# Four small edits in an fp32 decoder-layer kernel: v's sums in a paired PSUM buffer, a ninth matmul on ones, the third and fourth input blocks as DMAs of their own, and one weight piece split beside the second norm

## The chip, the core and the metric

The kernel runs on one core of a Trainium2 chip. The metric is the device time of one execution in microseconds (us); the median of several runs counts. The engines are PE (matmul; PEld is its weight load), DVE (VectorE), ACT (ScalarE), POOL (GpSimd) and SP (SyncE), which here issues all the DMAs.

## The reference, cut to what matters

```python
def hybrid_layer(x, ...):                       # x: (1, 256, 1024) float32
    h = rmsnorm(x, norm_mix_g)
    proj = h @ w_in                              # 1024 x (3*512 + 512 + 2*1024)
    q, k, v, u_pool, gate_logits = split(proj)
    q = rotary(rmsnorm(heads(q), q_norm_g)); k = rotary(rmsnorm(heads(k), k_norm_g))
    attn = causal_attention(q, k, heads(v))      # 8 heads of 64; one block of 256
    pooled = multiscale_pool_mixer(u_pool, w_pool, pool_scale)
    gates = sigmoid(gate_logits + b_gate)
    x = x + (gates[0] * (attn @ w_branch_attn) + gates[1] * (pooled @ w_branch_pool)) @ w_out
    h2 = rmsnorm(x, norm_ffn_g)
    gate, val = split(causal_conv3(h2 @ w_up))   # 1024 x 5632
    return x + (silu(gate) * val) @ w_down       # 2816 x 1024
```

All of it is float32. The kernel gets float32 precision by splitting every operand of a large product into a high and a low part and adding three products: high by high, high by low, low by high.

## The kernel before, in words

x is held transposed, 8 blocks k of 128 features by 256 tokens. The host packs block k of x and block k of q's weights side by side (256 + 512 columns a block, tile `xq`), with 8 columns of norm weights in front. A list of DMAs over `XCUTS` (L58, L191 to L196) loads them on SP's queue: blocks 0, 1, then 2-3, 4-5, 6-7. Behind them come k's first weights in two halves, a table `par`, and then whole chunks of 128 x 2048 (1 MB) in the fixed order of `order` (L107 on): k, v, p, g, ..., up, dn. A ring of four raw buffers holds the chunks; the DMA of the next chunk is issued when the last piece of the one in its buffer is split.

**Splitting.** A chunk is split in two pieces of 1024 columns: ACT rounds it (`high`, tile `hi_...`), DVE subtracts (`low`, tile `lo_...`). `ahead()` (L163) issues the next `high` and the next due `low` in the order of the chunks, wherever the program calls it. So the calls of `ahead()` are the plan: one more call moves every later piece one call forward, until the ring of four split buffers stops it (L145).

**Order.** At its end the program adds a dependency between neighbours on each engine, so every engine runs in written order.

**Warm-up.** Before the first data are there, `WARM` float32 matmuls of `ones` by `ones` run (L205). In the profile one of them is two MATMUL rows.

**Projections.** `project` (L274) makes q, k and v token-major: two PSUM banks (two tiles of 128 tokens by 512 columns), 8 blocks, 6 matmuls of 512 columns a block. The banks come from the pool `mm` of four in turn: warm-up, q0, q1, k0, k1, v0, v1, then u and the transposes. A bank is written again only when its readers are done. q0 and q1 are read by `norm_evacuate` (L287): ACT squares `q_q` and the DVE product `qg_q` (L295), which need the token norm `rtok` first. A second pool, `ps2`, has two buffers of two banks each; its first tile `ps_n1` holds the sums of the first norm and their spread (L242, L253), then attention's scores `ps_s` and probabilities `ps_p` use it, and at the end `ps_n2`, the second norm.

**FFN.** For each of 22 feature tiles i: two `ps_up` products (gate, value; 24 matmuls of 256 columns each), `normed`, `taps` and silu on DVE, ACT and POOL, and 24 matmuls of the down product of tile i - 3. Tiles 0 and 1 stand apart because the second norm is not there yet: tile 0 and half of tile 1 run first, `token_rms` (L242), `diagonal` (L249) and `spread_rms` (L253, L254) make `R2`, and only then can DVE empty the banks.

Of the kernel before, what the change touches and what calls it, by code (L numbers as in the profile page):

```python
# [8 lines left out]
F32 = mybir.dt.float32  # L9
# [5 lines left out]
P = 128  # L15
S = 256
NT = S // P
# [27 lines left out]
C_END = C_SIN + NT * ROPE  # L45

LAG = 3
WARM = 8
RAWBUFS = 4
WBUFS = 4  # L50
STAGGER = 1
# [3 lines left out]
FIRST = 2  # L55
HOME = 24
LEAD = 104
XCUTS = (1, 2, 4, 6, 8)  # L58


@with_exitstack
def hybrid_layer_kernel(ctx: ExitStack, tc: tile.TileContext, xq_d, par_d, wkv_d, wpg_d,
# [11 lines left out]
    ps2 = pairs.enter_context(tc.tile_pool(name="ps2", bufs=2, space=bass.MemoryType.PSUM))  # L74
    tmp = mixer.enter_context(tc.tile_pool(name="tmp", bufs=2))

    def bank(name):
        return mm.tile([P, 512], F32, tag="mm", name=name)
# [63 lines left out]
    def next_high():  # L142
        if at[0] < len(pieces):
            c, sl, first, _ = pieces[at[0]]
            if c - oldest() >= WBUFS:  # L145
                return
            at[0] += 1
            if first:
                his[c] = whi_p.tile([P, CH], F32R, tag="whi", name=f"hi_{order[c][0]}{c}")
                los[c] = wlo_p.tile([P, CH], F32R, tag="wlo", name=f"lo_{order[c][0]}{c}")  # L150
            high(his[c][:, sl], raw(c, sl))

    def next_low(eager=False):
        if at[1] < at[0] - STAGGER or at[0] == len(pieces) > at[1] or (at[1] < at[0] and eager):
            c, sl, _, last = pieces[at[1]]
            at[1] += 1
            low(los[c][:, sl], his[c][:, sl], raw(c, sl))
            if last and order[c][0] != "q":
                load()
# [3 lines left out]
    def ahead(upto=0):  # L163

        next_high()
        next_low()
        if at[1] - sum(p[0] < used[0] for p in pieces) < upto:
            next_high()
            next_low()

    def chunk(name):
        c = used[0]
        used[0] += 1
        spent.update(i for i in range(c) if order[i][0] != "dn")
        assert order[c][0] == name and all(p[0] > c for p in pieces[at[1]:]), (name, order[c][0])
        return his[c], los[c]
# [15 lines left out]
    cut = 0  # L192
    for k in XCUTS:
        end = KD + k * (S + AW)
# [9 lines left out]
    warm = bank("ps_warm")  # L204
    for i in range(WARM):  # L205
        nc.tensor.matmul(warm[:, 0:P], ones, ones, start=True, stop=True)
# [40 lines left out]
    def diagonal(rtok):  # L247
        for t in range(NT):
            nc.vector.tensor_scalar(diag[:, t, :], ident, rtok[:, t:t + 1], None, op0=ALU.mult)  # L249

    def spread_rms(pb, R):

        nc.tensor.matmul(pb, ones, diag.rearrange("p t c -> p (t c)"), start=True, stop=True)  # L253
        nc.vector.tensor_copy(R, pb)  # L254
# [16 lines left out]
            nc.vector.tensor_tensor(x2[:, 0:n * S], x2[:, 0:n * S], x2[:, n * S:2 * n * S], ALU.add)  # L271
            n //= 2

    def project(name, hook):  # L274
        pt = [bank(f"ps_{name}{t}") for t in range(NT)]
        for k in range(KD):
            if k % 4 == 0:
                hi, lo = chunk(name)
            sl = slice((k % 4) * 512, (k % 4 + 1) * 512)
            for sx, wx in ((xhi, hi), (xlo, hi), (xhi, lo)):  # L280
                for t in range(NT):
                    nc.tensor.matmul(pt[t], sx[:, k, t * P:(t + 1) * P], wx[:, sl], start=k == 0 and sx is xhi and wx is hi,  # L282
                                     stop=k == KD - 1 and wx is lo)
            hook(k)
        return pt
# [65 lines left out]

    qg, kg, stat = [], [], []
    ptq = project("q", on_q)
    ptk = project("k", on_k)
    ptv = project("v", on_v)
    for t in range(NT):
        nc.scalar.activation(vn[:, t, :], ptv[t], AF.Copy, scale=rtok1[:, t:t + 1])

# [204 lines left out]
    def tile_part(w, opers, c, ps, ks):  # L563
        hi, lo = w
        oph, opl = opers
        for k in ks:
            sl = slice(k * 256 + c * P, k * 256 + (c + 1) * P)
            mm3(ps[:, 0:S], (hi[:, sl], lo[:, sl]), (oph[:, k, :], opl[:, k, :]), k == 0, k == KD - 1)
# [38 lines left out]
    def normed(ps, f, name):  # L607

        u = tmp.tile([P, S], F32, tag="u", bufs=4, name=f"u_{name}")
        nc.vector.tensor_tensor(u, ps[:, 0:S], R2, ALU.mult)  # L610
        c = tmp.tile([P, S], F32, tag="cv", bufs=5, name=f"c_{name}")
        cw = par[:, C_CW + 2 * 2 * KF + f:C_CW + 2 * 2 * KF + f + 1]
        nc.scalar.activation(c, u, AF.Identity, scale=cw, bias=par[:, C_CB + f:C_CB + f + 1])
        return u, c
# [49 lines left out]
    ps = [bank("ps_up1_0")]  # L664
    tile_part(w, (hhi, hlo), 0, ps[0], range(KD))
    diagonal(rtok2)
    spread_rms(stat[:, 1, 0:S], R2)
    ug = normed(ps0[0], 0, "g0")
    uv = normed(ps0[1], KF, "v0")
# [107 lines left out]
```

## Time and profile before

| what | value |
|---|---|
| median of 3 runs | 342.76 us (342.73 to 342.76) |
| the profiled execution | 342.95 us; its span 341.1 us |
| around the span | 1.85 us |
| PE busy | 335.4 us, 98% of the span |
| DVE, ACT, POOL busy | 259.9, 198.1, 87.9 us |
| DMA | 62.76 MB, 184 GB/s mean |
| granted TensorE clock | 1.00 in every slice |

A row of a timeline gives the start from the start of the span, the duration, engine, line, operation, output<-input, shapes and count; in square brackets stands how long the engine was idle before and what ended that. The end of a matmul is modelled, and two matmuls overlap, so for PE the starts are what to compare: the start of the next row minus the start of this one is the time that its matmuls took.

### The profile page before, as it was taken

How to read it: one execution, taken by the hardware profiler on the slowest of the kernel's cores; microseconds unless marked ns; L12 is line 12 of the kernel's file. 1: busy time of each engine (PE TensorE's matmuls, PEld its weight loads, DVE VectorE, ACT ScalarE, POOL GpSimd, SP SyncE). 2: the span in 40 equal slices, each digit the busy share in tenths (PEclk: the TensorE clock that was granted, in tenths of full speed). 3: DMA queues.
4: the chain of work that ended last, by engine and by line, in shares of the span. 5: the costliest groups of instructions: out<-in, count | busy, mean ns of one | idle time of the engine just before them, and what ended most of it. 6: DMA issues, size and time to landing. Idle time of an engine off the chain costs nothing.

```text
span 341.1 us, 6723 instructions
## 1 busy us (share of the span) xinstructions
PE 335.4 (98%) x2736; PEld 324.6 (95%) x2736; DVE 259.9 (76%) x411; ACT 198.1 (58%) x319; POOL 87.9 (26%) x104
## 2 busy tenths in 40 slices
PE   8999999999999999999999999999999999999996
PEld 7887899999899999999999999999999999999995
DVE  4969989797587676698799977777777777777743
ACT  4956544635748954678276675655666666656420
POOL 1007992022203025022232322121212121212130
PEclk9999999999999999999999999999999999999999
DMA  7985543455372652376336674655556464642003
GB/s 266 422 343 225 195 179 121 157 171 219 113 254 110 221 175 102 123 249 246 125 123 218 265 246 142 243 159 213 190 181 223 149 246 133 240 142 107 0 2 123
DMA packets 10254, 62.76 MB, mean 184 GB/s; under 512 B 1136, under 2 KB 2288, under 8 KB 3312
## 3 DMA queue, kind: packets, MB, share of 16 engines
q1 hardware_dynamic: 10224, 62.34, 50.3%
q8 instruction: 21, 0.34, 0.4%
q14 instruction: 9, 0.07, 0.1%
HBM read 61.29 MB, written 1.05 MB: 183 GB/s over the span
## 4 chain that ended last, share of the span: by engine, by line
PE 85%; DVE 6%; DMA 4%; ACT 2%; SPq 1%; issue 1%; POOL 1%; POOLq 0%; ACTq 0%
PE ps_up L95 10%; PE ps_up L96 10%; PE ps_up L94 10%; PE ps_d L640 6%; PE ps_d L639 6%; PE ps_d L641 6%; PE ps_g L94 5%; PE ps_g L95 4%; PE ps_g L96 4%; DMA raw_k<-in_wkv 4%; PE ps_v L282 3%; PE ps_out L95 2%; PE ps_out L94 2%; PE ps_out L96 2%; PE ps_bp L94 1%; PE ps_ba L95 1%
## 5 line engine op out<-in xcount | busy, mean ns | idle before, releaser
L96 PE MATMUL ps_up<-hhi,lo_up 128*128 128x256 f32 x352 | 97.4, 277 | 0.6 <-DVE lo_up L86 0.6
L94 PE MATMUL ps_up<-hhi,hi_up 128*128 128x256 f32 x352 | 97.6, 277 | 0.0
L95 PE MATMUL ps_up<-hlo,hi_up 128*128 128x256 f32 x352 | 97.4, 277 | 0.0
L96 PEld LDWEIGHTS ps_up<-hhi,lo_up 128*128 128x128 f32 x352 | 66.1, 188 | 0.7 <-DVE lo_up L86 0.7
L95 PEld LDWEIGHTS ps_up<-hlo,hi_up 128*128 128x128 f32 x352 | 66.1, 188 | 0.2 <-DVE hlo L88 0.2
L94 PEld LDWEIGHTS ps_up<-hhi,hi_up 128*128 128x128 f32 x352 | 66.1, 188 | 0.0
L86 DVE TENSOR_TENSOR lo_up<-raw_up,hi_up 128x1024 fp32r<-128x1024 f32 x44 | 54.5, 1242 | 6.2 <-ACT hi_up L82 6.2
L639 PE MATMUL ps_d<-ah,hi_dn 128*128 128x256 f32 x176 | 48.6, 276 | 0.0
L640 PE MATMUL ps_d<-al,hi_dn 128*128 128x256 f32 x176 | 48.6, 276 | 0.0
L641 PE MATMUL ps_d<-ah,lo_dn 128*128 128x256 f32 x176 | 48.6, 276 | 0.0
L622 POOL TENSOR_TENSOR c_v<-c_g,c_v 128x256 f32<-128x256 f32 x22 | 16.2, 738 | 118.5 <-DVE c_v L605 118.5
L82 ACT ACTIVATE hi_up<-raw_up 128x1024 fp32r<-128x1024 f32 x44 | 45.0, 1046 | 0.0
L94 PE MATMUL ps_g<-xhi,hi_g 128*128 128x256 f32 x128 | 36.4, 285 | 0.0
L82 ACT ACTIVATE ah<-c_v 128x256 fp32r<-128x256 f32 x22 | 9.2, 418 | 45.8 <-POOL c_v L622 45.8
L96 PE MATMUL ps_g<-xhi,lo_g 128*128 128x256 f32 x128 | 35.7, 279 | 0.0
L95 PE MATMUL ps_g<-xlo,hi_g 128*128 128x256 f32 x128 | 35.7, 279 | 0.0
L641 PEld LDWEIGHTS ps_d<-ah,lo_dn 128*128 128x128 f32 x176 | 33.0, 188 | 0.0
L640 PEld LDWEIGHTS ps_d<-al,hi_dn 128*128 128x128 f32 x176 | 33.0, 188 | 0.0
L639 PEld LDWEIGHTS ps_d<-ah,hi_dn 128*128 128x128 f32 x176 | 33.0, 188 | 0.0
L86 DVE TENSOR_TENSOR lo_dn<-raw_dn,hi_dn 128x1024 fp32r<-128x1024 f32 x22 | 27.8, 1263 | 0.4 <-ACT hi_dn L82 0.4
L610 DVE TENSOR_TENSOR u_v<-ps_up,R 128x256 f32<-128x256 f32 x22 | 9.3, 421 | 22.7 <-PE ps_up L96 22.7
L94 PEld LDWEIGHTS ps_g<-xhi,hi_g 128*128 128x128 f32 x128 | 24.3, 190 | 0.9 <-issue 0.3
(183 smaller groups left out, 805.5 us busy)
## 6 DMA issues: line engine op xcount, KB each, us to landing
raw_up<-in_wup SPq DMA_DIRECT2D x22, 1024.0 KB, 4.8
raw_dn<-in_wdn SPq DMA_DIRECT2D x11, 1024.0 KB, 4.8
raw_g<-in_wpg SPq DMA_DIRECT2D x8, 1024.0 KB, 4.9
raw_o<-in_wout SPq DMA_DIRECT2D x4, 1024.0 KB, 4.8
xq<-in_xq SPq DMA_DIRECT2D x3, 768.0 KB, 7.4
raw_v<-in_wkv SPq DMA_DIRECT2D x2, 1024.0 KB, 14.0
raw_p<-in_wpg SPq DMA_DIRECT2D x2, 1024.0 KB, 6.3
raw_bp<-in_wbp SPq DMA_DIRECT2D x2, 1024.0 KB, 4.8
```

Of the source, the lines that this page charges most:

```text
L82: nc.scalar.activation(hi, src, AF.Copy, scale=scale)
L86: nc.vector.tensor_tensor(lo, src, hi.bitcast(F32), ALU.subtract)
L94: nc.tensor.matmul(out, sh, mh, start=start, stop=False, **kw)
L95: nc.tensor.matmul(out, sh, ml, start=False, stop=False, **kw)
L96: nc.tensor.matmul(out, sl, mh, start=False, stop=stop, **kw)
L282: nc.tensor.matmul(pt[t], sx[:, k, t * P:(t + 1) * P], wx[:, sl], start=k == 0 and sx is xhi and wx is hi, stop=k == KD - 1 and wx is lo)
L610: nc.vector.tensor_tensor(u, ps[:, 0:S], R2, ALU.mult)
L622: nc.gpsimd.tensor_tensor(uc[1], g[1], uc[1], ALU.mult)
L639: nc.tensor.matmul(o, hi[:, sl], acch[i], start=first, stop=False, skip_group_check=True)
L640: nc.tensor.matmul(o, hi[:, sl], accl[i], start=False, stop=False, skip_group_check=True)
L641: nc.tensor.matmul(o, lo[:, sl], acch[i], start=False, stop=i == KF - 1, skip_group_check=True)
```

## The change

Four edits. (1) `WARM` is 9 instead of 8. (2) `XCUTS` loads blocks 2 and 3 each with a DMA of its own. (3) v's two sums lie in one tile `ps_v` of the pool `ps2`, not in two banks of `mm`. (4) One more `ahead()` is called between `diagonal(rtok2)` and `spread_rms` of the second norm. Lines after L355 move by 2, after L666 by 3.

```diff
-WARM = 8
+WARM = 9
...
-XCUTS = (1, 2, 4, 6, 8)
+XCUTS = (1, 2, 3, 4, 6, 8)
...
-    def project(name, hook):
-        pt = [bank(f"ps_{name}{t}") for t in range(NT)]
+    def project(name, hook, pt=None):
+        pt = pt or [bank(f"ps_{name}{t}") for t in range(NT)]
...
-    ptv = project("v", on_v)
+
+    psv = ps2.tile([P, 2, 512], F32, tag="ps2", name="ps_v")
+    ptv = project("v", on_v, [psv[:, t, :] for t in range(NT)])
...
     tile_part(w, (hhi, hlo), 0, ps[0], range(KD))
     diagonal(rtok2)
+    ahead()
     spread_rms(stat[:, 1, 0:S], R2)
```

**PE, from the last matmuls of k to the first of v.** In square brackets stands which engines' semaphores an instruction waits for. Before:

```order
L282 MATMUL ps_k_239<-lo_k_216,xhi 128x512
L282 MATMUL ps_k_240<-lo_k_216,xhi 128x512
L282 MATMUL ps_v_347<-hi_v_253,xhi 128x512 [waits DVE_49,PE_49]
L282 MATMUL ps_v_348<-hi_v_253,xhi 128x512 [waits DVE_49,PE_49]
L282 MATMUL ps_v_347<-hi_v_253,xlo 128x512
L282 MATMUL ps_v_348<-hi_v_253,xlo 128x512
```

With the change:

```order
L282 MATMUL ps_k_241<-lo_k_218,xhi 128x512
L282 MATMUL ps_k_242<-lo_k_218,xhi 128x512
L282 MATMUL ps_v<-hi_v_255,xhi 128x512 [waits Activation_49]
L282 MATMUL ps_v<-hi_v_255,xhi 128x512
L282 MATMUL ps_v<-hi_v_255,xlo 128x512 x2
```

The waits of the first two matmuls of v for DVE (the readers of q0's and q1's banks) are gone; only the wait for ACT's high part of v's weights is left.

**DVE at the second norm** (`up27`, `up28` are the weight chunks of FFN tiles 2 and 3; `dn29` is the first down chunk). Before:

```order
L86 TENSOR_TENSOR lo_up28_1951<-raw_up28_1719,hi_up28_1950 128x1024
L249 TENSOR_SCALAR diag_168<-ident_111,rtok2_167 128x128 x2
L254 COPY R2_166<-ps_n2_1938 128x256
L610 TENSOR_TENSOR u_g0_1987<-ps_up0_0_1894,R2_166 128x256
L610 TENSOR_TENSOR u_v0_1991<-ps_up0_1_1895,R2_166 128x256
```

With the change:

```order
L86 TENSOR_TENSOR lo_up28_1952<-raw_up28_1720,hi_up28_1951 128x1024
L249 TENSOR_SCALAR diag_170<-ident_113,rtok2_169 128x128 x2
L86 TENSOR_TENSOR lo_up28_1952<-raw_up28_1720,hi_up28_1951 128x1024
L254 COPY R2_168<-ps_n2_1939 128x256
L612 TENSOR_TENSOR u_g0_1994<-ps_up0_0_1895,R2_168 128x256
```

On DVE the piece that the new call splits is the second half of `up28`; on ACT the same call issues the `high` of `dn29`'s first half, right behind that of `up28`.

**DVE at FFN tile 3** (`up30` is the weight chunk of tile 4, the fifth). Before:

```order
L610 TENSOR_TENSOR u_g3_2154<-ps_up3_0_2129,R2_166 128x256
L86 TENSOR_TENSOR lo_up30_2118<-raw_up30_1859,hi_up30_2117 128x1024
L610 TENSOR_TENSOR u_v3_2186<-ps_up3_1_2161,R2_166 128x256
L604 SCALAR_TENSOR_TENSOR c_g3_2156<-u_g3_2154,par_84,c_g3_2156 128x255
L605 SCALAR_TENSOR_TENSOR c_g3_2156<-u_g3_2154,par_84,c_g3_2156 128x254
L86 TENSOR_TENSOR lo_up30_2118<-raw_up30_1859,hi_up30_2117 128x1024
L86 TENSOR_TENSOR lo_up31_2194<-raw_up31_1954,hi_up31_2193 128x1024 x2
```

With the change:

```order
L612 TENSOR_TENSOR u_g3_2157<-ps_up3_0_2132,R2_168 128x256
L86 TENSOR_TENSOR lo_up30_2086<-raw_up30_1860,hi_up30_2085 128x1024
L612 TENSOR_TENSOR u_v3_2193<-ps_up3_1_2168,R2_168 128x256
L606 SCALAR_TENSOR_TENSOR c_g3_2159<-u_g3_2157,par_84,c_g3_2159 128x255
L607 SCALAR_TENSOR_TENSOR c_g3_2159<-u_g3_2157,par_84,c_g3_2159 128x254
L86 TENSOR_TENSOR lo_up31_2162<-raw_up31_1955,hi_up31_2161 128x1024 x2
L86 TENSOR_TENSOR lo_dn32_2235<-raw_dn32_1990,hi_dn32_2234 128x1024
```

Every piece has moved up one place: before `u_v3` now stands the second half of `up30`, where its first half stood. Two calls later the ring of split buffers holds both versions back at the same piece, and from there on the orders are the same.

## Rows read from the trace of the kernel before

**Rows 1.** The page, part 2: the granted TensorE clock in 40 slices, in tenths; part 4: the chain that ended last, shares of the span by engine.

```profile
PEclk9999999999999999999999999999999999999999
...
PE 85%; DVE 6%; DMA 4%; ACT 2%; SPq 1%; issue 1%; POOL 1%; POOLq 0%; ACTq 0%
```

**Rows 2.** PE's waits over the whole span: who waited for whom, us in total, times, longest.

```profile
PE ps_v L282 <- DVE qg_q L295: 0.6, 1, 0.6
PE ps_up L96 <- DVE lo_up L86: 0.6, 1, 0.6
PE ps_q L282 <- ACT hi_q L82: 0.2, 1, 0.2
```

**Rows 3.** Timeline of PE over the first blocks of q (block 0 at 5.02, block 1 at 7.17, block 2 at 8.66).

```profile
5.02 1.22 PE L282 MATMUL ps_q<-hi_q,xhi 128*128 128x512 f32 x2 [0.18 <-ACT hi_q L82]
6.04 0.83 PE L282 MATMUL ps_q<-hi_q,xlo 128*128 128x512 f32 x2
...
7.17 0.62 PE L282 MATMUL ps_q<-hi_q,xhi 128*128 128x512 f32 x2
...
8.09 0.62 PE L282 MATMUL ps_q<-lo_q,xhi 128*128 128x512 f32 x2
8.66 0.73 PE L282 MATMUL ps_q<-hi_q,xhi 128*128 128x512 f32 x2
9.23 0.62 PE L282 MATMUL ps_q<-hi_q,xlo 128*128 128x512 f32 x2
```

**Rows 4.** The warm-up's matmuls: count, duration in ns (min/median/max), first and last start in us.

```profile
L206 PE MATMUL ps_warm<-ones x16: 421/421/579, 1.1 to 4.4; 128*128 128x128 f32 x16
```

**Rows 5.** Timeline of ACT over the same stretch.

```profile
4.33 0.63 ACT L82 ACTIVATE hi_q<-xq 128x512 fp32r<-128x512 f32 x1 [2.11 <-DMA xq<-in_xq]
5.68 0.51 ACT L82 ACTIVATE xhi<-xq 128x256 fp32r<-128x256 f32 x1 [0.71 <-DMA xq<-in_xq]
6.09 0.61 ACT L82 ACTIVATE hi_q<-xq 128x512 fp32r<-128x512 f32 x1
7.58 0.51 ACT L82 ACTIVATE xhi<-xq 128x256 fp32r<-128x256 f32 x1 [0.88 <-DMA xq<-in_xq]
8.00 0.62 ACT L82 ACTIVATE hi_q<-xq 128x512 fp32r<-128x512 f32 x1
```

**Rows 6.** DMA issues of the first 40 us: count, KB each, median us from issue to landing.

```profile
xq<-in_xq SPq DMA_DIRECT2D x3, 768.0 KB, 7.4
...
xq<-in_xq SPq DMA_DIRECT2D x1, 384.0 KB, 4.5
```

**Rows 7.** Timeline of PE from the spread of the first norm to the first matmuls of v.

```profile
27.09 0.59 PE L253 MATMUL ps_n<-diag,ones 128*128 128x256 f32 x2
...
28.45 0.62 PE L282 MATMUL ps_k<-lo_k,xhi 128*128 128x512 f32 x2
28.91 0.40 PE L282 MATMUL ps_v<-hi_v,xhi 128*128 128x512 f32 x1
29.89 0.47 PE L282 MATMUL ps_v<-hi_v,xhi 128*128 128x512 f32 x1 [0.59 <-DVE qg_q L295]
```

**Rows 8.** Timeline of all engines, the rows that stand around v's products.

```profile
25.68 0.48 DVE L249 TENSOR_SCALAR diag<-ident,rtok 128x128 f32<-128x128 f32 x2 [0.83 <-POOL rtok L245]
...
29.00 0.74 DVE L295 SCALAR_TENSOR_TENSOR qg_q<-ps_q,rtok,par 128x512 f32<-128x512 f32 x1
...
30.79 3.40 DVE L86 TENSOR_TENSOR lo_v<-raw_v,hi_v 128x1024 fp32r<-128x1024 f32 x2
...
41.14 1.33 POOL L311 TENSOR_TENSOR qg_q<-ra_q,rb_q 128x128 f32<-128x128 f32 x1
...
46.39 1.03 PE L318 MATMUL ps_tq<-ident,qg_q 128*128 128x128 f32 x8
```

**Rows 9.** Timelines of DVE, ACT and PE between the second norm and FFN tile 4.

```profile
163.95 0.47 DVE L249 TENSOR_SCALAR diag<-ident,rtok 128x128 f32<-128x128 f32 x2
165.67 0.42 DVE L254 COPY R<-ps_n 128x256 f32<-128x256 f32 x1 [1.25 <-PE ps_n L253]
...
166.59 0.60 ACT L613 ACTIVATE c_g<-u_g,par 128x256 f32<-128x256 f32 x1 [4.37 <-DVE u_g L610]
...
179.80 1.72 DVE L86 TENSOR_TENSOR lo_up<-raw_up,hi_up 128x1024 fp32r<-128x1024 f32 x1
...
182.84 1.22 DVE L86 TENSOR_TENSOR lo_up<-raw_up,hi_up 128x1024 fp32r<-128x1024 f32 x1
...
183.28 0.28 PE L95 MATMUL ps_up<-hlo,hi_up 128*128 128x256 f32 x1
184.11 0.38 PE L96 MATMUL ps_up<-hhi,lo_up 128*128 128x256 f32 x1 [0.55 <-DVE lo_up L86]
184.33 0.28 PE L94 MATMUL ps_up<-hhi,hi_up 128*128 128x256 f32 x1
```

**Rows 10.** Timeline of PE, five matmuls of 256 columns: between the first two stand 62 others without a wait, between the next two 44; the last is PE's last matmul.

```profile
148.10 0.28 PE L94 MATMUL ps_out<-mh,hi_o 128*128 128x256 f32 x1
...
155.52 0.28 PE L94 MATMUL ps_out<-mh,hi_o 128*128 128x256 f32 x1
...
166.17 0.28 PE L94 MATMUL ps_up<-hhi,hi_up 128*128 128x256 f32 x1
...
171.27 0.28 PE L94 MATMUL ps_up<-hhi,hi_up 128*128 128x256 f32 x1
...
337.58 0.28 PE L641 MATMUL ps_d<-ah,lo_dn 128*128 128x256 f32 x1
```

## The prediction

> **What bounds the kernel now.** Read the shares of the chain that ended last first: PE is 85% of it [rows 1]. So the kernel is one long row of matmuls, and only two things can move the end: matmuls added or taken away, and places where PE stands still. PE's waits come next, and there are only three behind the warm-up: v's sums for DVE's `qg_q`, one `ps_up` for a low part, q for its first high part [rows 2]. The profile counts them from the modelled end of the matmul before, so it understates them. The timelines give the true price by starts: the reader should see what a matmul costs when nothing is in the way, and subtract. 512 columns take 0.23 us each: block 1 of q at 7.17 and its last pair at 8.09 stand four matmuls and 0.92 us apart [rows 3]. 256 columns take either 0.118 us (63 in 7.42) or 0.113 us (45 in 5.10), according to the stretch [rows 10].
>
> **The third and fourth blocks apart.** Blocks 2 and 3 now come in one DMA of 768 KB [rows 6]. ACT begins block 2 at 7.58, when they land; block 1 landed at 5.68 [rows 5]. PE pays for it twice: its last pair of block 1 needs 0.46 us but the next pair starts 0.57 later, at 8.66, and that pair takes another 0.57 (its first weights were not loaded behind another matmul) [rows 3]. Together 0.22 us. With a DMA of its own, block 2 should land about halfway between 5.68 and 7.56, at 6.6; ACT is free at 6.70 and needs 0.42 + 0.62 us by its own starts [rows 5], so the high part is there at 7.74, and PE would be ready at 8.55. Slack 0.8 us. Gain 0.22.
>
> The other end of the price: 384 KB blocks could be slower carriers. The one in the trace landed 1.35 us behind the block ahead of it (4.33 to 5.68), 768 KB took 1.90 [rows 5, 6]. Two at 1.35 make 2.70, so everything behind them could land 0.8 us later. Block 2 would still be in time; k's second chunk would not quite. The first norm hangs on it by way of ACT and DVE: `diag` ends at 26.16 [rows 8], 0.8 later at 26.96, while PE comes to its matmul at 27.09 - 0.22 = 26.87 [rows 7]. With its weights loaded late that is up to 0.3 us lost. So this edit lies between -0.22 and +0.3, a DMA that lands no earlier being 0 in between. I take -0.22, the end that the measured landings are nearest to: the queue was never empty there, and the first 384 KB block stands at the start of the stream. The Trainium skill, "DMA: Bandwidth & Descriptors", section Bandwidth, speaks against this edit: it asks for DMAs of 1 MB or more, since smaller ones reach a smaller share of the bandwidth. Rows 5 and 6 agree in direction, and by the page the total would be that of the +0.3 end, 341.5.
>
> The extra issue on SP takes its turn while the queue holds megabytes, so it costs nothing as long as that backlog stands.
>
> **The ninth matmul on ones.** It is two more rows of 0.22 us ((4.4 - 1.1)/15) [rows 4]: the last starts at 4.85 and frees the array at 5.06, where q's first starts at 5.02 today [rows 3]. But q's first needs its own weight load then, which can run beside the warm-up. Cost between 0 and 0.26 (the last one's modelled end, 4.85 + 0.42, against 5.02). I take 0, the spacing being the measured thing. What it could give back is a rival below.
>
> **v's sums in `ps2`.** PE starts v's first matmul at 28.91 and its second at 29.89, when DVE's `qg_q` of q1 (29.00 + 0.74) has freed the bank [rows 7, 8]. 0.98 instead of 0.23: 0.75 us. In `ps2` the buffer has not been used, so the whole 0.75 goes. Everything of PE from here on is then 0.22 + 0.75 = 0.97 us earlier, and what is late next? v's second low parts end at 34.19 [rows 8]; PE needs the later of them in block 6 of v, 40 matmuls of 0.23 behind the start at 28.69, at 37.9. POOL ends the second `qg_q` at 42.47, its transposes come at 46.39 - 0.97 = 45.42 [rows 8]. Both covered. Two banks fewer are drawn from `mm`, so later tiles get other banks but the same distance of four; the transposes of q now wait for the readers of k's banks instead of v's, which ended earlier. Attention's first scores take the buffer of the first norm, 30 us after its last reader. No cost.
>
> **One more `ahead()`.** At tile 4 PE starts one matmul at 183.28, the next at 184.11 and the one after at 184.33: 0.83 + 0.22 instead of 2 x 0.113, that is 0.83 us, ended by the second half of `up30`'s low part (182.84 to 184.06) [rows 9]. With the change this piece stands where the first half stood, 179.80 to 181.52, and PE wants it at 183.40: slack 1.9 us, so the stall goes whole. What pays? DVE does the same work; the new piece, 1.22 us, fills the time before `R2`'s copy in which DVE stood idle for 1.25 (from 164.42 to 165.67), and ACT's stands in an idle time of 4.37 [rows 9]. If the piece takes 1.72 as another did [rows 9], `R2` and the emptying of tile 0's banks come 0.5 us later, at 167.0 instead of 166.5; PE, with 24 matmuls from 165.3, wants that bank at 168.0. Covered. The DMA for the next chunk is issued some 8 us earlier, into a queue that is not full. Afterwards the plan is the old one, in which PE never waited again.
>
> **The sum.** -0.22 - 0.75 - 0.83 = -1.80 us. The profiled execution took 342.95, which gives 341.15; the median of the runs lies 0.19 below the profiled one, so I forecast **341.0 us**, 0.5% faster. A measurement of this kernel tells a change of 0.2% (0.7 us) from none.
>
> **Rivals.**
>
> *The clock rises earlier.* The granted clock reads 1.00 in every slice (a digit of 9 is 0.9 or more) [rows 1], but the starts say otherwise: warm-up and q's first two pairs run at the lower level, 1.2 GHz (1.02 us for a pair with its weights), and from about 6.5 us on at 2.4 GHz (0.23 a matmul) [rows 3, 4]. Between the warm-up's last start at 4.4 and q's the array idles some 0.4 us; the ninth matmul fills that. If the rise then came before 5 us, block 1 could start when its high part is there, at 6.70 [rows 5] instead of 7.17: 0.47 us more, **340.5**. For it: only the filled gap. Against it: the unbroken warm-up from 1.05 to 4.6 did not raise it. The Trainium skill, "TensorE: Matmul & The Clock Gate", Part 1, says that the array is throttled until it has been active, and that the moment shifts from run to run; by the first the rival has a chance, the second the trace does not bear out (three runs within 0.03 us). Chance 0.10.
>
> *Part of it is not paid.* The split DMA costs instead of saving (341.5), or one of the two large waits only moves: v's sums or tile 4 (341.7 to 341.8). For it: POOL and DVE durations vary (a low part took 1.2 to 1.7). Together 0.14, still faster than 342.1.
>
> *Nothing to be seen.* Both large waits come back behind the next late thing, 342 to 343. It would take several covers of 0.5 to 3 us failing. 0.07.
>
> *Slower by the cadence.* The FFN's 256-column matmuls run at 0.113 us, the stage before them at 0.118 [rows 10], same shapes, no wait. The step falls at the second norm's spread at 165. What sets the cadence the rows do not show; the change moves PE's arrival there and takes away the wait at 184. If the FFN kept the slower cadence from there to PE's last start at 337.58, it would be 172.3/0.1133 = 1520 matmuls times 0.0045 = 6.8 us: **347.8**. It decides at that one matmul, nothing in between would tell. Against it: the wait at 184 left the cadence as it was, and the order on PE is unchanged. 0.07. The other way round, more stretches at 0.113, would give something below 340.3: 0.04.
>
> **How the numbers follow.** Forecast 0.58, clock 0.10, partly 0.14, nothing 0.07, slower 0.07, quicker cadence 0.04. The range of 340.3 to 342.0 takes in the first three and the bounds of the unknown prices; it leaves out 0.18. Faster 0.58 + 0.10 + 0.14 + 0.04 = 0.86, same 0.07, slower 0.07.
>
> **What would show it.** In the profile after: block 2's first matmul right behind block 1's last pair, 0.46 and not 0.57; no wait in front of `ps_v`, its first two starts 0.23 apart; no wait of `ps_up` for a low part; `R2`'s copy within 0.1 us of where PE's spread ends; starts of 256 columns still 0.113 apart behind the second norm. Any new line in PE's waits, k's or v's low parts above all, would make a term wrong; 0.118 in the FFN would make the whole prediction wrong.

## The result and the profile after

The change takes **340.34 us** (median of 5 runs, 340.31 to 341.04) against 342.76 us: ratio 0.9937, interval 0.9925 to 0.995. Run once more beside the experiments it gave 340.49 (6 runs) and the same ratio. Its eleven runs lie in two places: seven from 340.31 to 340.58, four from 340.98 to 341.04. With three early runs and two late ones in the first five, the median is that of the early place. Runs of 347 to 350 us are left out of all comparisons and ratios here: they are 43 of the 118 runs of kernels that have the wait at FFN tile 4 (before, u_ahead, o_cuts, o_v, w1_before) and none of the 64 runs of kernels without it, and what causes them was not studied.

The profiled execution took 340.33 us, span 338.6. PE's waits (who waits for whom: us in total, times, longest) have two lines left; of those of before [rows 2], v's and tile 4's are gone:

```profile
PE ps_warm L206 <- DVE ones L180: 1.1, 1, 1.1
PE ps_q L282 <- ACT hi_q L82: 0.6, 1, 0.6
```

The timeline of PE at the start answers [rows 3, 4] (start, duration, engine, line, operation, tiles, count):

```profile
3.77 0.92 PE L206 MATMUL ps_warm<-ones 128*128 128x128 f32 x6
...
5.33 0.74 PE L282 MATMUL ps_q<-hi_q,xhi 128*128 128x512 f32 x2 [0.64 <-ACT hi_q L82]
5.91 0.63 PE L282 MATMUL ps_q<-hi_q,xlo 128*128 128x512 f32 x2
...
6.84 0.63 PE L282 MATMUL ps_q<-hi_q,xhi 128*128 128x512 f32 x2
...
7.77 0.62 PE L282 MATMUL ps_q<-lo_q,xhi 128*128 128x512 f32 x2
8.23 0.62 PE L282 MATMUL ps_q<-hi_q,xhi 128*128 128x512 f32 x2
```

Block 2 follows block 1's last pair after 0.46 us, without a gap. But block 0 differs as well: six matmuls in 1.51 us from 5.33, where before they took 2.15 from 5.02. Warm-up rows start 0.21 apart up to 3.97 and 0.11 apart from there: the clock went from 1.2 to 2.4 GHz at 4.0 us, inside the warm-up and ahead of the ninth matmul's two rows (4.31, 4.42). Before, it rose near 6.5 us. The profile's granted clock reads 1.00 on both sides of the step (3.0 to 3.9 and 4.0 to 4.5 us), so here and below the moment of the rise is read from where the starts come closer.

The timeline of ACT answers [rows 5]:

```profile
5.62 0.51 ACT L82 ACTIVATE xhi<-xq 128x256 fp32r<-128x256 f32 x1 [0.34 <-DMA xq<-in_xq]
...
6.59 0.51 ACT L82 ACTIVATE xhi<-xq 128x256 fp32r<-128x256 f32 x1
7.01 0.61 ACT L82 ACTIVATE hi_q<-xq 128x512 fp32r<-128x512 f32 x1
7.74 0.51 ACT L82 ACTIVATE xhi<-xq 128x256 fp32r<-128x256 f32 x1
```

Block 2 is begun at 6.59, without a wait, and its high part is there at 7.62, ahead of PE at 8.23. Further on, the timeline of PE (v, the stretch on `ps_u`, the second norm, tile 4, the end) answers [rows 7, 9, 10]:

```profile
28.37 0.62 PE L282 MATMUL ps_v<-hi_v,xhi 128*128 128x512 f32 x2
28.82 0.62 PE L282 MATMUL ps_v<-hi_v,xlo 128*128 128x512 f32 x2
...
39.36 0.28 PE L94 MATMUL ps_u<-xhi,hi_p 128*128 128x256 f32 x1
...
44.70 0.28 PE L96 MATMUL ps_u<-xhi,lo_p 128*128 128x256 f32 x1
...
163.38 0.60 PE L253 MATMUL ps_n<-diag,ones 128*128 128x256 f32 x2
...
181.62 0.28 PE L95 MATMUL ps_up<-hlo,hi_up 128*128 128x256 f32 x1
181.74 0.28 PE L96 MATMUL ps_up<-hhi,lo_up 128*128 128x256 f32 x1
181.85 0.28 PE L94 MATMUL ps_up<-hhi,hi_up 128*128 128x256 f32 x1
...
335.08 0.28 PE L643 MATMUL ps_d<-ah,lo_dn 128*128 128x256 f32 x1
```

v's first pair goes without a gap, and so does tile 4. `ps_u` runs at 0.114 us a matmul (the second row of it stands 47 behind the first). From tile 4 to the end the distance is that of before (153.2 us). The same 47 matmuls of `ps_u` took 5.53 us before, 0.118 each; timeline of PE in the kernel before:

```profile
40.74 0.28 PE L94 MATMUL ps_u<-xhi,hi_p 128*128 128x256 f32 x1
...
46.27 0.28 PE L96 MATMUL ps_u<-xhi,lo_p 128*128 128x256 f32 x1
```

The timeline of DVE shows the moved pieces of tile 4: the extra one ends at 163.90, `R`'s copy starts 0.03 behind the modelled end of PE's spread (163.38 + 0.60), and the half that PE waited for is done at 179.86, 1.88 ahead of its use at 181.74.

```profile
162.68 1.22 DVE L86 TENSOR_TENSOR lo_up<-raw_up,hi_up 128x1024 fp32r<-128x1024 f32 x1
164.01 0.42 DVE L254 COPY R<-ps_n 128x256 f32<-128x256 f32 x1
...
178.15 1.71 DVE L86 TENSOR_TENSOR lo_up<-raw_up,hi_up 128x1024 fp32r<-128x1024 f32 x1
```

Laying the starts of the same matmul of both traces side by side shows where PE's last start came forward by 2.50 us: 0.55 in q, 0.83 at v, 0.20 in `ps_u`, 0.07 ahead of the second norm, 0.84 at tile 4.

### The profile page after: what moved, and what is told of

It is laid out like the page before. It is cut to its first block, busy times and chain, and to the rows that moved or that the text cites. A ratio compares the mean times of both kernels' runs of the same rounds, so it can differ in the third digit from the quotient of the medians.

```text
span 338.6 us, 6730 instructions
## 1 busy us (share of the span) xinstructions
PE 333.6 (99%) x2738; PEld 323.8 (96%) x2738; DVE 259.9 (77%) x411; ACT 198.3 (59%) x319; POOL 86.4 (26%) x104
## 3 DMA queue, kind: packets, MB, share of 16 engines
HBM read 61.29 MB, written 1.05 MB: 184 GB/s over the span
## 4 chain that ended last, share of the span: by engine, by line
PE 97%; DMA 1%; ACT 0%; DVE 0%; issue 0%; ACTq 0%
PE ps_up L95 12%; PE ps_up L96 12%; PE ps_up L94 12%; PE ps_d L643 6%; PE ps_d L642 6%; PE ps_d L641 6%; PE ps_g L94 5%; PE ps_g L95 4%; PE ps_g L96 4%; PE ps_q L282 3%; PE ps_k L282 3%; PE ps_v L282 3%; PE ps_out L95 2%; PE ps_out L94 2%; PE ps_out L96 2%; PE ps_bp L94 1%
```

## Experiments

The question is why the time came out lower than forecast and in two places. **Theory A**: the moment of the clock's rise differs from execution to execution, with eight matmuls on ones as with nine. In the kernel before two waits hide it: block 2's high part, and at v `qg_q`, whose end no work of PE sets. The change removes both, so the moment now shows in the time, and the gains of single edits don't add. **Rival B**: the ninth matmul brings the rise forward, and the gains add.

### The change with one edit undone

```
u_warm    -WARM = 9                     +WARM = 8
u_cuts    -XCUTS = (1, 2, 3, 4, 6, 8)   +XCUTS = (1, 2, 4, 6, 8)
u_v       -ptv = project("v", on_v, [psv[:, t, :] for t in range(NT)])
          +ptv = project("v", on_v)
u_ahead   -    ahead()          (behind diagonal(rtok2))
```

**u_warm.** 

> The change without the ninth matmul on ones. Theory A (the moment at which the clock rises differs from execution to execution whatever the warm-up, and the ninth matmul costs and brings nothing): times in the same two groups as the change, 340.3 and 341.0 us. Rival B (the ninth matmul brings the rise forward to 4 us): all executions late, 341.0 or more, and in the profile 512-column starts in the first pairs of q 0.45 us apart up to about 6.5 us.

Measured: 340.53 us, 340.34 to 342.18 in 10 runs (six at most 340.60); ratio 0.994, interval 0.992 to 0.996. Six of ten are as short as the change's early ones, so the early rise does not need the ninth matmul: B falls. (o_v and o_ahead below have eight, and their profiles show an early rise.) The profiled execution (340.77) happens to be of a late rise. Timeline of PE:

```profile
5.17 1.22 PE L282 MATMUL ps_q<-hi_q,xhi 128*128 128x512 f32 x2 [0.34 <-ACT hi_q L82]
6.19 0.80 PE L282 MATMUL ps_q<-hi_q,xlo 128*128 128x512 f32 x2
6.83 0.63 PE L282 MATMUL ps_q<-lo_q,xhi 128*128 128x512 f32 x2
...
8.67 0.62 PE L282 MATMUL ps_q<-hi_q,xhi 128*128 128x512 f32 x2
```

Block 0 runs at 1.2 GHz until about 6.5; block 2 is 0.44 later than in the change (8.67 for 8.23), PE's last start 0.44, and the time 0.44. So in this execution the late rise moves the end one for one. Neither theory has the two runs at 342.1 and 342.2, and no profile shows one.

**u_cuts.** 

> The change with blocks 2 and 3 in one DMA again. Theory A (an early rise of the clock pays only if block 2's high part is there early): block 2 starts at 8.66 whether the clock rose at 4 or at 6.5 us, so one group of times, 340.3 + 0.43 to 0.55 = 340.75 to 340.9 us. Rival B (the split is worth only the 0.22 of the prediction, the rest is the clock's whenever it rises): 340.5 to 340.6, and a second group 0.5 above it.

Measured: 341.03 us (340.95 to 341.45), ratio 0.9947, interval 0.9933 to 0.996: five of six runs within 0.17 us and one 0.33 above them, 0.54 to 0.69 above the change by the medians, a little more than A's figure. The clock rose at 4.6 us in the profile, and block 2 still starts at 8.67:

```profile
7.81 0.63 PE L282 MATMUL ps_q<-lo_q,xhi 128*128 128x512 f32 x2
8.67 0.73 PE L282 MATMUL ps_q<-hi_q,xhi 128*128 128x512 f32 x2 [0.24 <-ACT hi_q L82]
```

Block 2 starts 0.44 later than in the change (8.67 for 8.23), and its first pair takes 0.57 instead of 0.46: the split is worth 0.55 once the rise is early.

**u_v.** 

> The change with v's sums in the common banks again. Theory A (PE then waits at v for DVE's qg_q, whose end near 29.74 us is set by the first norm's DMA, ACT and DVE work and not by PE, so that what was gained in q is swallowed there): +0.83 + 0.55 = +1.38, 341.7 us, and one group of times only; up to 341.9 if the stretch on ps_u falls back to 0.118 us a matmul. Rival B (the three gains add): +0.83, 341.15, and a second group at 341.9.

Measured: 341.99 us (341.77 to 342.31, 9 runs), ratio 0.9973, interval 0.9962 to 0.9985. A's 1.4 is in the profile (PE's last start 1.41 later than the change's), B's 341.15 is not; the median lies 0.1 above A's highest figure. Timeline of PE, then of DVE:

```profile
28.48 0.40 PE L282 MATMUL ps_v<-hi_v,xhi 128*128 128x512 f32 x1
29.90 0.47 PE L282 MATMUL ps_v<-hi_v,xhi 128*128 128x512 f32 x1 [1.03 <-DVE qg_q L295]
```

```profile
29.01 0.75 DVE L295 SCALAR_TENSOR_TENSOR qg_q<-ps_q,rtok,par 128x512 f32<-128x512 f32 x1
```

PE arrives 0.43 earlier than before [rows 7] and goes on at the same 29.90: `qg_q` starts at 29.01, against 29.00 in [rows 8]. The gain in q has become a longer wait.

**u_ahead.** 

> The change without the extra ahead(). Theory A (the wait at tile 4 comes back, 0.83 us, and nothing else changes): 341.15 us, with a second group 0.7 us above it, 341.85. Rival B (PE arrives 1.6 us earlier at tile 4 while DVE's low part hangs on DVE's own work, so the wait is longer than before): up to 342.8.

Measured: 341.41 to 341.60 us (4 runs), ratio 0.9961, interval 0.9946 to 0.9976. Timeline of DVE and of PE:

```profile
181.56 1.22 DVE L86 TENSOR_TENSOR lo_up<-raw_up,hi_up 128x1024 fp32r<-128x1024 f32 x1
```

```profile
182.00 0.28 PE L95 MATMUL ps_up<-hlo,hi_up 128*128 128x256 f32 x1
182.84 0.39 PE L96 MATMUL ps_up<-hhi,lo_up 128*128 128x256 f32 x1 [0.56 <-DVE lo_up L86]
```

The wait is back with its old price (0.84 from start to start, 0.83 before), not longer: DVE's half ends at 182.78 here and 184.06 in [rows 9], so DVE had come forward with PE. PE's last start is 1.23 behind the change's. Of the other 0.4 us, 0.36 stand at the start: 0.15 behind block 1's high part, which came late in this execution (ACT began block 1 at 5.81 us, 5.62 in the change), and 0.21 because q and k ran at 0.2333 us a matmul for a while (below). So the time lies between A's two figures, for reasons other than the clock; B falls.

### One edit alone, and the change once more

```
o_cuts    -XCUTS = (1, 2, 4, 6, 8)      +XCUTS = (1, 2, 3, 4, 6, 8)
o_v       -ptv = project("v", on_v)
          +psv = ps2.tile([P, 2, 512], F32, tag="ps2", name="ps_v")
          +ptv = project("v", on_v, [psv[:, t, :] for t in range(NT)])
o_ahead   +    ahead()          (behind diagonal(rtok2))
```

**o_cuts.** 

> The kernel before with blocks 2 and 3 in DMAs of their own, nothing else. Theory A (PE's earlier end of q is swallowed at v, where it waits for qg_q anyway until near 29.74 us): no change, 342.7 to 342.8 us; in the profile q's blocks earlier by 0.2 to 0.55, and v's second start within 0.1 of 30.20, where it is in the kernel before. Rival B (the gains add): -0.22 to -0.55, 342.2 to 342.55.

Measured: 342.66 to 343.83 us (10 runs), ratio 1.0005, interval 0.9996 to 1.0015: no change, as A has it. Timeline of PE, and of ACT and DVE by their own:

```profile
7.99 0.62 PE L282 MATMUL ps_q<-lo_q,xhi 128*128 128x512 f32 x2
8.44 0.62 PE L282 MATMUL ps_q<-hi_q,xhi 128*128 128x512 f32 x2
...
28.58 0.39 PE L282 MATMUL ps_v<-hi_v,xhi 128*128 128x512 f32 x1
30.10 0.47 PE L282 MATMUL ps_v<-hi_v,xhi 128*128 128x512 f32 x1 [1.14 <-DVE qg_q L295]
```

```profile
17.14 1.06 ACT L82 ACTIVATE hi_k<-raw_k 128x1024 fp32r<-128x1024 f32 x1 [0.75 <-DMA raw_k<-in_wkv]
```

```profile
29.21 0.74 DVE L295 SCALAR_TENSOR_TENSOR qg_q<-ps_q,rtok,par 128x512 f32<-128x512 f32 x1
```

q ends 0.33 earlier and v's second matmul starts 0.21 *later*. ACT's wait for `raw_k` is what sets it: it ended at 16.93 before and at 17.14 here, and `qg_q` starts 12.07 behind it in both; in the other three profiles that have this wait of v (u_v, o_ahead, w1_before) it is 12.07 or 12.08. So PE's lead in q does not reach the end of that chain.

**o_v.** 

> The kernel before with v's sums in the second-norm pair's buffer, nothing else. Theory A: the wait at v goes, -0.83, or -1.03 if the stretch on ps_u also runs at 0.113 us a matmul: 341.75 to 341.95 us. Rival B (0.75 as predicted): 342.0. The rival of the prediction that the wait only moves to v's low parts: 342.7, with a wait of ps_v for lo_v.

Measured: 341.94 us (341.74 to 341.99, 9 runs), ratio 0.9971, interval 0.9961 to 0.9982. The time alone does not tell A's 341.75 to 341.95 from B's 342.0; the profile does. Against that of before, PE is 0.84 earlier behind v's first pair, 0.18 more by the end of `ps_u` (which ran at 0.114), 0.09 more elsewhere. No wait of `ps_v` is left.

**o_ahead.** 

> The kernel before with the extra ahead() alone. Theory A (a wait behind all the others, independent of them): -0.83, 341.9 us, no wait of ps_up for a low part. Rival B (a part of the 0.83 came from PE's earlier arrival, so that alone it brings less): 342.2 or more, with a wait left at tile 4.

Measured: 341.92 us (341.74 to 342.11), ratio 0.9975, interval 0.9965 to 0.9985, as A has it. Its profile has an early rise (block 1 at 6.72), and the kernel hides it: block 2 at 8.59, v's second matmul at 29.83, 0.06 earlier than before. `ps_u` ran at 0.114 here too, with v in the common banks, so v's place is not what sets that.

**again.** 

> The changed kernel once more. Theory A (the moment at which the clock rises differs between executions, and now sets the time): every time of 340.3 to 341.1 us goes with one moment; if this profile is of a late execution, the last start of PE is later by what q's first two blocks are later, and by nothing else. Rival B (the two groups come from the stretches at 0.118 or 0.113 us a matmul): the difference builds up behind 30 us.

Measured: 340.37 to 340.58 (four) and 340.98, 341.00; the profiled one took 340.37. It fell in the first group, so the later one still has no profile. The rise came at another moment than in the first profile: the last warm-up rows stand 0.21 apart (four in 1.06; six took 0.92 there), q's first pairs 0.46.

```profile
4.20 1.06 PE L206 MATMUL ps_warm<-ones 128*128 128x128 f32 x4
```

A rise between 4.8 and 5.3 is as good as one at 4.0, since q's first high part is not there sooner. PE's last start differs by 0.01.

### The rise, later and with a longer warm-up

```
w1_after   -WARM = 9   +WARM = 1        w11_after  -WARM = 9   +WARM = 11
w1_before  -WARM = 8   +WARM = 1
```

**w1_after.** 

> The change with one matmul on ones in place of nine, so that TensorE stands idle from about 1.5 us to q's first at 5.2 to 5.4. Both theories: q's first blocks run at the lower clock, and the rise comes later than in any execution so far. Theory A (nothing hides the moment of the rise in the changed kernel): each microsecond at 1.2 GHz costs 0.47 (two rows of 0.43 to 0.45 us where 0.23 would do); with a rise at 8 us 0.47 x (8.0 - 5.3) = 1.3, so 341.6 us, more for a later rise, and the last start of PE later by exactly what q is later. Rival B (the moment of the rise is hidden behind something else further on): 340.3 to 341.0 us.

Measured: 342.38 us (341.65 to 343.29, 12 runs), ratio 0.9991, interval 0.9979 to 1.0002: all that the change had won is gone. Timeline of PE in the profiled execution (341.92):

```profile
6.10 1.05 PE L282 MATMUL ps_q<-hi_q,xlo 128*128 128x512 f32 x2
6.96 1.05 PE L282 MATMUL ps_q<-lo_q,xhi 128*128 128x512 f32 x2
7.81 0.95 PE L282 MATMUL ps_q<-hi_q,xhi 128*128 128x512 f32 x2
8.60 0.63 PE L282 MATMUL ps_q<-hi_q,xlo 128*128 128x512 f32 x2
```

A pair starts every 0.85 us until the clock rises near 8.4. PE is then 1.29 behind the change, and 1.57 at the end, the rest being a stretch of q and k at 0.2333 us a matmul. The figure of 1.3 was for a rise at 8 us and a q that starts at 5.3. Here q starts at 5.08, 0.25 ahead of the change, and is 1.29 behind at 8.60: 1.54 lost, where 0.47 x (8.4 - 5.1) gives 1.55.

**w1_before.** 

> The kernel before with one matmul on ones in place of eight. Theory A (the moment of the rise is covered twice, by block 2 at 8.66 us and by the 0.75 us at v): with a rise at 8 us q ends 0.47 x (8.0 - 6.47) = 0.7 later and v's second matmul starts at 29.9 as before, so 342.75 to 342.95 us; only what q is late beyond 0.75 shows in the end. Rival B (no cover): the same loss as the change has with one matmul, 343.5 or more.

Measured: 343.10 to 343.90 us (7 runs), ratio 1.0019, interval 1.0008 to 1.003. By the ratio 0.65 us are lost (0.3 to 1.0): more than A's 0 to 0.2, less than the 1.9 to 2.0 that the change loses. So there is a cover, but it does not hide all. Timeline of PE in the profiled execution, which took 348.86 us and is read here up to v alone:

```profile
29.38 0.39 PE L282 MATMUL ps_v<-hi_v,xhi 128*128 128x512 f32 x1
30.11 0.47 PE L282 MATMUL ps_v<-hi_v,xhi 128*128 128x512 f32 x1 [0.34 <-DVE qg_q L295]
```

The clock rises near 7.9 us there, and v's first matmul starts 0.47 later than before, but PE still waits for `qg_q` there. The second starts 0.22 later, and that is not PE's doing: ACT's wait for `raw_k` ended at 17.14 instead of 16.93. So in this execution a rise near 8 is hidden whole, as A has it. That the 0.65 us of the seven runs come from later rises is an estimate, not shown: the cover is 0.55 at block 2 (u_cuts) and 0.76 at v (o_ahead: 28.84 to 29.83, less 0.23), 1.3 in all, and of 1.9 to 2.0 that leaves 0.6 to 0.7. It would take rises later than 8.4, the moment in the profile of w1_after; nine of that kernel's twelve runs took longer than the profiled one.

**w11_after.** 

> The change with eleven matmuls on ones in place of nine: at the lower clock the last of 22 rows would start at 5.7 us, behind q's first at 5.3. Theory A (the moment of the rise does not hang on the warm-up): two groups of times again, 340.35 and 341.0, the later one with q's first 0.4 later still. Rival B (a TensorE that is never idle ahead of q has the rise early every time): one group at 340.3 to 340.4 us.

Measured: 340.24, 340.28, 340.40, and 340.80, 341.08, 341.28; ratio 0.9936, interval 0.9922 to 0.9949. Three early runs and three later ones, as A has it, though the later three spread over half a microsecond. In the profile (340.80) the warm-up's rows hold the array until q starts at 5.76, 0.43 late, and the end is 0.48 late. The rise comes between 5.7 and 6.2, though PE had worked without a break from 1.05. So more warm-up does not make the rise early every time.

The moments of the rise in all profiles with eight or nine matmuls on ones, the first always at 1.05 us:

| kernel | rise, us | kernel | rise, us |
|---|---|---|---|
| after | 4.0 | again | 4.8 to 5.3 |
| u_cuts | 4.6 | before | 6.5 |
| u_ahead | 4.8 to 5.1 | u_warm | 6.5 |
| u_v | 5.8 | o_cuts | 6.1 |
| o_v | 5.0 to 5.4 | o_ahead | 4.4 to 5.2 |

## Why the prediction was right, and where it was not

The forecast was 341.0 us in a range of 340.3 to 342.0; the median is 340.34, or 0.66 below and just inside the range. The mechanisms of the three terms were right, every sign in "what would show it" came, and no new wait did. One size was off by a factor of 2.5, since the clock rose earlier than the prediction held likely, and some stretches ran at the quicker cadence. Both pull the same way, and that the sum of the two stayed within the range is in part luck.

- **Blocks apart, -0.22.** The term that was mis-sized: -0.55 in the profile. The prediction took the start of block 2 from an execution in which the clock rose at 6.5, when PE arrived hardly ahead of the high part (8.55 for 8.61). With an earlier rise PE waits there longer, and the split pays more (u_cuts). With a late one it pays little: in u_warm's profile v starts 0.11 earlier than before.
- **The clock as a rival, 340.5 with a chance of 0.10.** An early rise is what both profiles of the change show, and by their times seven of its eleven runs had it, but not by the mechanism given: u_warm does it without the filled gap. The step that failed is "the second the trace does not bear out (three runs within 0.03 us)". Equal times could show only that the end did not depend on the moment: two waits behind q hid it. And three runs were few: 42 later runs of the same kernel go from 342.56 to 343.60 us. The Trainium skill says in "TensorE: Matmul & The Clock Gate", Part 1, that the moment shifts from run to run, by half a microsecond either way. The table above agrees that it shifts, but spans 2.5 us, and the measurement decides.
- **The edit's other end, +0.3.** Its cause came in part, its price did not. Each of the two DMAs was to take 1.35 us; in the change ACT began block 2 0.97 behind block 1, and block 3 1.15 behind block 2. From ACT's start on block 1 to the end of its wait for `raw_k` it is 11.25 to 11.27 us in the five profiles without the split, and 11.27 to 12.06 in the eight with it (mean 11.53, 11.45 in the change). So the split does make later chunks land later, by 0 to 0.8 us. In the change no wait of PE hangs on that; of o_cuts' 0.21 us it is 0.15. The Trainium skill asks for DMAs of 1 MB or more ("DMA: Bandwidth & Descriptors", section Bandwidth). These landings agree with its direction.
- **Ninth matmul, 0.** Right (u_warm).
- **v's sums, -0.75.** -0.83: the third matmul of v also stood 0.31 instead of 0.23 behind the second. The second's weights were loaded only at 29.86, when the wait ended, and the third's behind them at 29.97. The prediction had counted just this at block 2 and not here. That the wait goes whole, and that no low part of v is late next, held (o_v).
- **The extra `ahead()`, -0.83.** -0.84, with a slack of 1.88 where 1.9 was worked out. Alone it brings the same (o_ahead).
- **The sum.** By PE's starts it is -2.5 instead of -1.8: 0.33 more at the blocks, 0.08 more at v and 0.27 from the cadence. Adding the gains held for the three edits together, and would have failed for one alone: the split by itself is worth nothing (o_cuts), without v's move it is lost again (u_v).
- **The cadence.** The FFN kept 0.113. The rival's other direction (chance 0.04) came in small: 0.20 in `ps_u`, 0.07 ahead of the second norm. It is not this change's: w1_before, which has none of the four edits, runs `ps_u` at 0.114 too, and before and o_cuts alone at 0.118. The 0.118 that the rival feared for the FFN occurs in one profile, w1_before's, from the matmul behind tile 4's wait to the end; the four others that have this wait stay at 0.113. What sets the cadence stays open.

Open, too: no profile caught an execution of the change near 341.0. That it is a still later rise is argued from u_warm (0.44 late, 0.44 lost), not shown. A late rise together with a stretch of q and k at 0.2333 us a matmul (0.21 in u_ahead, 0.28 in w1_after) would fit the 0.65 us as well.

## What to carry to other kernels

Before adding gains along one engine's queue, ask of each later wait whose work sets its end: a wait that ends with another engine's chain swallows everything gained ahead of it, and removing it pays out the earlier gains as well. Equal run times say that a fluctuation doesn't reach the end, not that there is none; a change that removes the cover makes it visible. So read where such a fluctuation stands (here the clock's rise) in the profile before taking a duration from it.

## What the runs showed of the hardware

The distance from one matmul's start to the next has two values for the same shape, and each lasts for long stretches. 42 matmuls of 512 columns take 9.61 us in the change and 9.80 in u_ahead, over the same part of q and k. Timeline of PE, of the change and of u_ahead:

```profile
11.89 0.62 PE L282 MATMUL ps_q<-lo_q,xhi 128*128 128x512 f32 x2
...
21.50 0.62 PE L282 MATMUL ps_k<-lo_k,xhi 128*128 128x512 f32 x2
```

```profile
12.07 0.63 PE L282 MATMUL ps_q<-lo_q,xhi 128*128 128x512 f32 x2
...
21.87 0.40 PE L282 MATMUL ps_k<-lo_k,xhi 128*128 128x512 f32 x1
```

That is 0.2289 and 0.2333 us, 4.4 ns apart; the 256-column matmuls have 0.1133 and 0.118, 4.5 ns apart [rows 10]. So it is about the same amount for each matmul at both sizes, and not a rate: as a share it is 1.9% and 4%. No run showed what switches it.
